# Row turns moved among the first products, and the remainder columns put first in each pair

## The chip, the core and the metric

The kernel runs on one core of one Trainium2 chip. The metric is the device time of one execution in microseconds. "Before" is the median of nine executions. The span of a profile is the time from the first to the last recorded instruction of one profiled execution; about 1.8 us of that execution's own time lie outside it.

## The reference

```
qkv = matmul(x, w_qkv)          # x: (16, 512, 768) f32, w_qkv: (768, 2304) f32
q, k, v = qkv[..., :768], qkv[..., 768:1536], qkv[..., 1536:]
out = stack([q, k, v])          # (3, 16, 512, 768) f32
```

It is one product of 8192 rows by 768 by 2304 columns, with the result split into three equal column groups.

## The kernel before, in words

**Tiling.** The 8192 rows are 32 pairs of two 128-row tiles, pairs numbered from 0. The contraction of 768 is six k-tiles of 128 (KT = 6, KH = 3); k-tile j holds every sixth row of the weights. The 2304 columns are two groups q = 0, 1 of 1024 columns (each two blocks c = 0, 1 of CB = 512) and 256 remainder columns (REM) between them.

**Pairs 0 to 2, direct.** While the weights arrive, these pairs are computed plainly in bf16: `block(q, c, w, groups, cast_next)` runs the products of one column block for all six row tiles, with `groups` as the written-out order of (k-tiles, row tiles). Their rows are loaded as they lie (`load_rows`), cast to bf16 by `cast_rows` (half of each row tile on DVE, half on ACT, or both on DVE with `two=False`), and turned by `turn_rows`: six PE transposes against the identity `eye` into a PSUM bank, then two copies into `xb`. `busy(n)` issues n products of zeros on PE. `cast_k(j)` casts one weight k-tile of the first block. `rem(p)` computes the 256 remainder columns of a pair: twelve 256-column matmuls, one ACT copy to `orem`, one store on SP's queue.

**Pairs 3 to 31, seven products.** For these the two row tiles, the two halves of the contraction and the two blocks of a column group make a two by two by two block product, computed with seven products (Strassen's scheme) for each q. The sums of weights (`sum_w`) and of rows (`sums_x`, on POOL) are fp32r; products 1 and 2 are bf16 and direct. The next pair's rows come in by `load_x` (four quarters, two on SP's queue and two on another), are turned on DVE in 32 by 32 blocks (`transpose`), cast by POOL to `xb` (`round_x`) and summed. `two(a, b, early)` is one pair, with quads a and b for q = 0 and 1. Its order on PE is: product 1 of a and b, `rem`, product 2 of both, product 6 of both, products 5, 7 of a, 5, 7 of b, then 4, 3 of a and 4, 3 of b. `early()` issues the next pair's transposes and sums and the loads of the pair after it. Products 1, 6, 7 and 4 share one PSUM bank per quad (`u.x`), copied out by ACT between them; products 5 and 3 share another (`u.y`), which DVE adds into the output after product 7 and again after product 3. `store_quad` issues two stores per quad on SP's queue. `last(a, b)` is pair 31 with finer stores.

**What sets the order.** The engines' orders are as written; each engine and each issuing queue runs its own list in order and waits on semaphores. Every transfer is given one of eight completion semaphores in turn, and the program makes a transfer's issue wait for the landing of the transfer eight places earlier. PSUM has eight banks, taken in turn (`ps_pool`, bufs=8); row buffers `xin` have three, outputs `o` five, `orem` two.

**Lines of the profile.** L212 products of the seven-product loop; L262 remainder products; L385 direct products; L167 transposes on PE; L365 products of zeros; L145/L149 DVE and L147 ACT halves of casts and turned copies; L413 `cast_k`; L426/L427 casts of the remainder weights; L130 DVE transpose; L175 POOL cast; L226, L233, L239, L243 ACT copies after products 1, 6, 7, 4; L230, L240, L246 DVE adds after products 2, 7, 3; L272/L273 copy and store of `rem`; L89 weight loads; L141 row loads; L126 quarters of `load_x`; L253/L254 and L257/L258 stores of q = 0 and 1.

Of the kernel before, what the change touches and what calls it, by code (L numbers as in the profile page):

```python
# [10 lines left out]
def kernel(  # L11
# [20 lines left out]
    nc = tc.nc  # L32
    P = 128
# [3 lines left out]
    K = H  # L37
    N3 = w_qkv.shape[1]
    KT = K // P
    KH = KT // 2  # L40
    KC = K // 4
    NP = M // (2 * P)
    CB = 512
    REM = N3 - 4 * CB
    Q_OFF = (0, 2 * CB + REM)
    R_OFF = 2 * CB
    fp32 = mybir.dt.float32
    f32r = mybir.dt.float32r
    bf16 = mybir.dt.bfloat16
    ident = mybir.ActivationFunctionType.Identity  # L50
# [9 lines left out]
    tq_pool = ctx.enter_context(tc.tile_pool(name="tq", bufs=2))  # L60
# [6 lines left out]
    xb_pool = ctx.enter_context(tc.tile_pool(name="xb", bufs=4))  # L67
    rem_pool = ctx.enter_context(tc.tile_pool(name="rem", bufs=1))
    s_pool = ctx.enter_context(tc.tile_pool(name="s", bufs=2))
    ps_pool = ctx.enter_context(tc.tile_pool(name="ps", bufs=8, space=bass.MemoryType.PSUM))  # L70
# [4 lines left out]
    eye = w_pool.tile([P, 176], bf16, name="eye")[:, :P]  # L75
    w_rem = [w_pool.tile([P, KH, REM], bf16, name="w_rem0"), None]

    b1 = [w_pool.tile([P, KT, CB], bf16, name=f"b1_{q}") for q in range(2)]
# [8 lines left out]
    def load_w(dst, j0, nj, off, cols):  # L87
        rows = w_qkv.rearrange("(p j) n -> p j n", j=KT)
        nc.sync.dma_start(dst, rows[:, j0:j0 + nj, off:off + cols])  # L89

    stage = {}

    def load_blocks(q, c, nj=KH):
        if q == 0:
            t = tq_pool.tile([P, KT, CB], fp32, name="st0", tag="tq")
            for j in range(0, KT, nj):
                load_w(t[:, j:j + nj], j, nj, Q_OFF[q] + c * CB, CB)
            stage[q, 0, c], stage[q, 1, c] = t[:, :KH, :], t[:, KH:, :]
        else:
            for h in range(2):  # L100
                t = st_pool.tile([P, KH, CB], fp32, name="st1", tag="st")
                load_w(t[:], h * KH, KH, Q_OFF[q] + c * CB, CB)
                stage[q, h, c] = t[:]
# [11 lines left out]
    xin, xf, xb, sr = {}, {}, {}, {}  # L115
# [22 lines left out]
    def load_rows(p):  # L138
        xin[p] = xin_pool.tile([P, 2, K], fp32, name="xin")
        rows = x_flat[p * 2 * P:(p + 1) * 2 * P, :]  # L140
        nc.sync.dma_start(xin[p][:], rows.rearrange("(r m) k -> m r k", m=P))  # L141

    def copy_halves(dst, src, two):

        nc.vector.tensor_copy(out=dst[0], in_=src[0])  # L145
        if two:
            nc.scalar.activation(dst[1], src[1], ident)  # L147
        else:
            nc.vector.tensor_copy(out=dst[1], in_=src[1])  # L149

    xc = {}

    def cast_rows(p, two=True):
        src = xin.pop(p)
        xc[p] = s_pool.tile([P, 2, K], bf16, name="xc", tag="s")
        for r in range(2):
            halves = (slice(0, K // 2), slice(K // 2, K))
            copy_halves([xc[p][:, r, n] for n in halves], [src[:, r, n] for n in halves], two)

    def turn_rows(p, two=True):  # L160
        c = xc.pop(p)
        xb[p] = xb_pool.tile([P, KT, 2 * P], bf16, name="xb", tag="xb")
        for r in range(2):
            cols = c[:, r, :].rearrange("m (p j) -> m j p", j=KT)
            ps = ps_pool.tile([P, KT, P], bf16, name="ps")
            for j in range(KT):
                nc.tensor.transpose(ps[:, j, :], cols[:, j, :], eye)  # L167
            ks = (slice(0, KH), slice(KH, KT))
            copy_halves(
                [xb[p][:, n, r * P:(r + 1) * P] for n in ks], [ps[:, n, :] for n in ks], two  # L170
            )

    def round_x(p):
        xb[p] = xb_pool.tile([P, KT, 2 * P], bf16, name="xb", tag="xb")
# [42 lines left out]
    def bank():  # L217
        return ps_pool.tile([P, CB], fp32, name="ps")

    def do(u, n):  # L220
        c11, c12 = u.o[:, 0, :CB], u.o[:, 0, CB:]
        c21, c22 = u.o[:, 1, :CB], u.o[:, 1, CB:]
        if n == 1:
            u.x = bank()
            product(u, 1, u.x, True)
            nc.scalar.activation(c11, u.x[:], ident)  # L226
        elif n == 2:
            u.z = bank()
            product(u, 2, u.z, True)
            nc.vector.tensor_tensor(c11, c11, u.z[:], op=add)  # L230
        elif n == 6:
            product(u, 6, u.x, False)
            nc.scalar.activation(c12, u.x[:], ident)  # L233
        elif n == 5:
            u.y = bank()
            product(u, 5, u.y, True)
        elif n == 7:
            product(u, 7, u.x, False)
            nc.scalar.activation(c22, u.x[:], ident)  # L239
            nc.vector.tensor_tensor(c22, c22, u.y[:], op=add)  # L240
        elif n == 4:
            product(u, 4, u.x, False)
            nc.scalar.activation(c21, u.x[:], ident)  # L243
        elif n == 3:
            product(u, 3, u.y, False)
            nc.vector.tensor_tensor(c12, c12, u.y[:], op=add)  # L246

    def rows_of(s, p, lo, hi):
        return out_flat[s, p * 2 * P:(p + 1) * 2 * P, lo:hi].rearrange("(r m) n -> m r n", m=P)
# [10 lines left out]
    def rem_row(p, r, ps):  # L260
        for j in range(KT):
            nc.tensor.matmul(  # L262
                ps, xb[p][:, j, r * P:(r + 1) * P], w_rem[j // KH][:, j % KH, :],
                start=(j == 0), stop=(j == KT - 1), skip_group_check=True,
            )

    def rem(p):
        ps = ps_pool.tile([P, 2, REM], fp32, name="ps")
        for r in range(2):
            rem_row(p, r, ps[:, r, :])  # L270
        o = or_pool.tile([P, 2, REM], fp32, name="orem")
        nc.scalar.activation(o[:], ps[:], ident)  # L272
        nc.sync.dma_start(rows_of(1, p, R_OFF - H, R_OFF - H + REM), o[:])  # L273

    def two(a, b, early):

        do(a, 1)
        do(b, 1)
        early()
        rem(a.p)  # L280
        do(a, 2)
        do(b, 2)
        do(a, 6)
        do(b, 6)
        do(a, 5)
        do(a, 7)
        do(b, 5)
        do(b, 7)
        do(a, 4)
        do(a, 3)  # L290
        store_quad(a)
        do(b, 4)
        do(b, 3)
        store_quad(b)
# [52 lines left out]
    load_rows(0)  # L347
    nc.scalar.activation(tiny[:], zero[:, :1], ident)
    make_identity(nc, eye)
    load_rows(1)  # L350
    load_blocks(0, 0, 1)
    st_rem = o_pool.tile([P, KT, REM], fp32, name="str", tag="o")
    load_w(st_rem[:], 0, KT, R_OFF, REM)
    load_rows(2)
    load_blocks(0, 1)
    load_blocks(1, 0)
    load_blocks(1, 1)
    load_x(3, nc.sync)
# [16 lines left out]
    def block(q, c, w, groups, cast_next):  # L375


        ps = {}
        for js, tiles in groups:
            for n in tiles:  # L380
                p, r = divmod(n, 2)
                if n not in ps:
                    ps[n] = bank()
                for j in js:
                    nc.tensor.matmul(  # L385
                        ps[n][:], xb[p][:, j, r * P:(r + 1) * P], w[:, j, :],
                        start=(j == 0), stop=(j == KT - 1), skip_group_check=True,
                    )
                if KT - 1 not in js:
                    continue  # L390
                if r == 0:
                    cast_next(p)
                u = quads[q][p]
                nc.scalar.activation(u.o[:, r, c * CB:(c + 1) * CB], ps[n][:], ident)
                if c == 1 and r == 1:
                    store_quad(u)

    def halves(tiles):
        return [(range(h * KH, (h + 1) * KH), tiles) for h in range(2)]


    singles = [((0, ), (0, 1)), ((1, ), (0, 1)), ((0, 1), (2, 3))]
    singles += [((j, ), range(4)) for j in range(2, KT)]

    act, dve = nc.scalar, nc.vector
    def cast_k(j):
        dve.tensor_copy(out=b1[0][:, j, :], in_=stage[0, j // KH, 0][:, j % KH, :])

    def cast_next(q, c, w):
        return lambda p: p < 2 and cast(q, p, c, w, act)  # L410

# [2 lines left out]

    nothing = lambda p: None
    busy(11)
    cast_rows(0)
    turn_rows(0)
    busy(4)
    cast_rows(1)  # L420
    cast_k(0)
    cast_k(1)
    turn_rows(1)
    for j in range(2, KT):
        cast_k(j)
    act.activation(w_rem[1][:], st_rem[:, KH:], ident)  # L426
    dve.tensor_copy(out=w_rem[0][:], in_=st_rem[:, :KH])  # L427
    bt0 = bt_pool.tile([P, KT, CB], bf16, name="bt")
    bt1 = bt_pool.tile([P, KT, CB], bf16, name="bt")

    block(0, 0, b1[0], singles, nothing)
    rem(0)
    rem(1)
    cast_rows(2, False)
    turn_rows(2, False)
    block(0, 0, b1[0], halves((4, 5)), nothing)
    for h in range(2):
        cast(0, h, 1, bt0, dve)
    for n in range(1, 5):
# [61 lines left out]
```

## Time and profile before

| | us |
|---|---|
| median of 9 executions | 362.58 (362.48 to 363.1) |
| the profiled execution, own time | 362.66 |
| its span | 360.9 |
| PE busy (matmuls) | 354.6 |
| DVE, ACT, POOL busy | 224.7, 182.5, 173.8 |
| bytes moved | 108.08 MB, 299 GB/s over the span |
| granted TensorE clock | 1.0 |

Busy time is the sum of an engine's recorded instructions; PE's matmuls are pipelined and their ends are modelled, so 98% does not say that PE ran at its best. In lines of the timeline the columns are start, length, engine, source line, operation, tile written and tile read, shape, count, and in square brackets the idle time of the engine just before with what ended it. A name ending in q (SPq, ACTq) is the engine's issuing queue. Times of single landings come from the trace's records of semaphore updates by the DMA engines.

### The profile page before, as it was taken

To read this page: it belongs to the slowest core of one execution; us is meant where nothing else is said; L and a number is where in the kernel's file an instruction comes from. 1 tells how busy PE (TensorE), PEld (TensorE's weight loads), DVE (VectorE), ACT (ScalarE), POOL (GpSimd) and SP (SyncE) were. 2 spreads that over 40 slices of the span, in tenths; PEclk is the share of its full clock that TensorE was granted. 3 is DMA by queue.
4 is the path that set the end of the run, shared out by engine and by line. 5 is a ranking of instruction groups with operands and counts; after the bars stand their busy time and mean duration, and the time that the engine had idled before them with its cause. 6 is when DMAs were issued, how large, how long until landed. Compare 5 with 4: busy or idle time off the path is not lost.

```text
span 360.9 us, 5253 instructions
## 1 busy us (share of the span) xinstructions
PE 354.6 (98%) x1797; PEld 250.5 (69%) x1797; DVE 224.7 (62%) x239; ACT 182.5 (51%) x304; POOL 173.8 (48%) x180
## 2 busy tenths in 40 slices
PE   8999999999999999999999999999999999999995
PEld 3644577777777777777777777777777777777763
DVE  3489836765566675566675556676556676556642
ACT  4557554545454545444445444545545454545452
POOL 0000961646664445665445665444666444666410
PEclk9999999999999999999999999999999999999999
DMA  7999869988898999999899999988989899999666
GB/s 296 404 389 370 311 226 359 320 294 293 277 329 302 290 275 296 276 317 317 278 286 284 287 299 314 293 276 291 295 280 324 296 300 271 297 272 337 264 262 232
DMA packets 80617, 108.08 MB, mean 299 GB/s; under 512 B 4816, under 2 KB 60368, under 8 KB 80592
## 3 DMA queue, kind: packets, MB, share of 16 engines
q1 hardware_dynamic: 65184, 96.35, 80.9%
q10 hardware_dynamic: 15408, 11.41, 9.6%
q8 instruction: 14, 0.23, 0.3%
q14 instruction: 11, 0.09, 0.1%
HBM read 32.24 MB, written 75.50 MB: 299 GB/s over the span
## 4 chain that ended last, share of the span: by engine, by line
PE 97%; ACT 1%; ACTq 0%; DVE 0%; issue 0%
PE ps L212 75%; PE ps L262 11%; PE ps L385 9%; PE ps L365 1%; PE ps L167 0%; ACT o L243 0%; ACTq L303 0%; ACT xb L147 0%; ACT orem L317 0%; DVE xb L145 0%; ACT xc L147 0%; ACTq L319 0%; DVE zero L346 0%; ACTq L317 0%
## 5 line engine op out<-in xcount | busy, mean ns | idle before, releaser
L212 PE MATMUL ps<-t,s 128*128 128x512 f32 x696 | 173.8, 398 | 0.0
L212 PEld LDWEIGHTS ps<-t,s 128*128 128x128 f32 x696 | 130.7, 188 | 29.8
L175 POOL CAST xb<-xf 128x1536 bf16<-128x1536 f32 x29 | 43.8, 1510 | 167.8 <-DVE xf L130 133.8
L240 DVE TENSOR_TENSOR o<-o,ps 128x512 f32<-128x512 f32 x58 | 39.9, 688 | 91.1 <-ACT o L239 91.1
L130 DVE STREAM_TRANSPOSE xf<-xin 128x1536 f32<-128x1536 f32 x29 | 85.5, 2949 | 3.2 <-DMA out_dram<-orem 2.0
L212 PE MATMUL ps<-b,xb 128*128 128x512 bf16 x348 | 84.9, 380 | 0.0
L239 ACT ACTIVATE o<-ps 128x512 f32<-128x512 f32 x58 | 34.7, 598 | 44.2 <-PE ps L212 44.2
L212 PEld LDWEIGHTS <-xb 128*128 128x128 bf16 x348 | 31.7, 98 | 35.6 <-issue 7.3
L233 ACT ACTIVATE o<-ps 128x512 f32<-128x512 f32 x58 | 34.8, 600 | 42.1 <-PE ps L212 39.4
L246 DVE TENSOR_TENSOR o<-o,ps 128x512 f32<-128x512 f32 x58 | 39.9, 688 | 21.4 <-PE ps L212 20.2
L212 PE MATMUL ps<-b,s 128*128 128x512 f32 x174 | 48.7, 389 | 0.0
L262 PE MATMUL ps<-w_rem,xb 128*128 128x256 bf16 x384 | 47.2, 273 | 0.0
L243 ACT ACTIVATE o<-ps 128x512 f32<-128x512 f32 x58 | 34.7, 598 | 24.1 <-PE ps L212 21.3
L226 ACT ACTIVATE o<-ps 128x512 f32<-128x512 f32 x58 | 34.6, 597 | 23.8 <-DVE o L246 20.6
L262 PEld LDWEIGHTS <-xb 128*128 128x128 bf16 x384 | 37.4, 98 | 11.2 <-issue 0.5
L230 DVE TENSOR_TENSOR o<-o,ps 128x512 f32<-128x512 f32 x58 | 36.5, 670 | 4.9 <-PE ps L212 3.6
L212 PEld LDWEIGHTS ps<-b,s 128*128 128x128 f32 x174 | 32.7, 188 | 6.8
L184 POOL TENSOR_TENSOR s<-s,xf 128x384 fp32r<-128x384 f32 x29 | 30.0, 1035 | 2.3
L183 POOL TENSOR_TENSOR s<-xf 128x384 fp32r<-128x384 f32 x29 | 30.9, 1065 | 0.0
L185 POOL TENSOR_TENSOR s<-xf 128x384 fp32r<-128x384 f32 x29 | 29.5, 1017 | 0.0
L187 POOL TENSOR_TENSOR s<-xf,s 128x384 fp32r<-128x384 f32 x29 | 29.4, 1014 | 0.0
L272 ACT ACTIVATE orem<-ps 128x512 f32<-128x512 f32 x31 | 18.5, 598 | 20.7 <-PE ps L262 20.7
(36 smaller groups left out, 128.7 us busy)
## 6 DMA issues: line engine op xcount, KB each, us to landing
out_dram<-o SPq DMA_DIRECT2D x62, 768.0 KB, 4.9
out_dram<-o SPq DMA_DIRECT2D x65, 256.0 KB, 4.2
xin<-in_x_dram SPq DMA_DIRECT2D x62, 192.0 KB, 6.9
xin<-in_x_dram ACTq DMA_DIRECT2D x54, 192.0 KB, 4.3
out_dram<-orem SPq DMA_DIRECT2D x31, 256.0 KB, 5.8
st<-in_w_qkv_dram SPq DMA_DIRECT2D x6, 768.0 KB, 13.3
xin<-in_x_dram SPq DMA_DIRECT2D x3, 768.0 KB, 5.6
st<-in_w_qkv_dram SPq DMA_DIRECT2D x6, 256.0 KB, 6.0
```

What stands on the lines that cost most here:

```text
L130: nc.vector.transpose(t[:].rearrange("p j (g b) -> p g j b", b=G), xin.pop(p)[:].rearrange("p g (a j) -> p g j a", a=G),)
L175: nc.gpsimd.tensor_copy(out=xb[p][:], in_=xf[p][:])
L212: nc.tensor.matmul(ps[:], lhs[j], rhs[j], start=(start and j == 0), stop=(j == KH - 1), skip_group_check=True,)
L226: nc.scalar.activation(c11, u.x[:], ident)
L230: nc.vector.tensor_tensor(c11, c11, u.z[:], op=add)
L233: nc.scalar.activation(c12, u.x[:], ident)
L239: nc.scalar.activation(c22, u.x[:], ident)
L240: nc.vector.tensor_tensor(c22, c22, u.y[:], op=add)
L243: nc.scalar.activation(c21, u.x[:], ident)
L246: nc.vector.tensor_tensor(c12, c12, u.y[:], op=add)
L262: nc.tensor.matmul(ps, xb[p][:, j, r * P:(r + 1) * P], w_rem[j // KH][:, j % KH, :], start=(j == 0), stop=(j == KT - 1), skip_group_check= ...
L385: nc.tensor.matmul(ps[n][:], xb[p][:, j, r * P:(r + 1) * P], w[:, j, :], start=(j == 0), stop=(j == KT - 1), skip_group_check=True,)
```

## The change

Five things are different.

1. `cast_rows` and `turn_rows` become `cast_row(p, r)` and `turn_row(p, r)`, for one row tile at a time. The instructions are the same.
2. For pair 1, the casts are interleaved with the casts of k-tiles 0 and 1. The turn of its first tile (`third_row`) comes after the products of k-tile 0 with pair 0, and that of its second tile (`fourth_row`) after those of k-tile 1. The casts of the other k-tiles and of the remainder weights are issued inside these functions, so `block` accepts functions among its groups.
3. For pair 2, the cast and turn of its first tile come after the remainder products of pair 0, and those of its second tile after the remainder products of pair 1. The two tiles' products of the first block then run one tile after the other, six k-tiles each, where they ran in two halves of three.
4. The remainder weights are loaded in two transfers instead of one. The other loads keep their order (`load_blocks(0, 1, KH)` passes the value that was the default).
5. In `two`, `rem(a.p)` moves from behind product 1 and `early()` to the front of the pair. This holds for pairs 3 to 30.

```diff
-    def cast_rows(p, two=True):
-        src = xin.pop(p)
-        xc[p] = s_pool.tile([P, 2, K], bf16, name="xc", tag="s")
-        for r in range(2):
...
-    def turn_rows(p, two=True):
-        c = xc.pop(p)
-        xb[p] = xb_pool.tile([P, KT, 2 * P], bf16, name="xb", tag="xb")
-        for r in range(2):
...
+    def cast_row(p, r, two=True):
+        if r == 0:
+            xc[p] = s_pool.tile([P, 2, K], bf16, name="xc", tag="s")
+        halves = (slice(0, K // 2), slice(K // 2, K))
+        copy_halves([xc[p][:, r, n] for n in halves], [xin[p][:, r, n] for n in halves], two)
+
+    def turn_row(p, r, two=True):
+        if r == 0:
+            xb[p] = xb_pool.tile([P, KT, 2 * P], bf16, name="xb", tag="xb")
+        cols = xc[p][:, r, :].rearrange("m (p j) -> m j p", j=KT)
+        ps = ps_pool.tile([P, KT, P], bf16, name="ps")
+        for j in range(KT):
+            nc.tensor.transpose(ps[:, j, :], cols[:, j, :], eye)
...
     def two(a, b, early):
+        rem(a.p)
         do(a, 1)
         do(b, 1)
         early()
-        rem(a.p)
         do(a, 2)
...
-    load_w(st_rem[:], 0, KT, R_OFF, REM)
+    for h in range(2):
+        load_w(st_rem[:, h * KH:(h + 1) * KH], h * KH, KH, R_OFF, REM)
     load_rows(2)
...
-        for js, tiles in groups:
+        for group in groups:
+            if callable(group):
+                group()
+                continue
+            js, tiles = group
...
     busy(4)
-    cast_rows(1)
+    cast_row(1, 0)
     cast_k(0)
+    cast_row(1, 1)
     cast_k(1)
-    turn_rows(1)
-    for j in range(2, KT):
-        cast_k(j)
-    act.activation(w_rem[1][:], st_rem[:, KH:], ident)
-    dve.tensor_copy(out=w_rem[0][:], in_=st_rem[:, :KH])
+
+    def third_row():
+        turn_row(1, 0)
+        cast_k(2)
+
+    def fourth_row():
+        turn_row(1, 1)
+        for j in range(3, KT):
+            cast_k(j)
+        dve.tensor_copy(out=w_rem[0][:], in_=st_rem[:, :KH])
+        act.activation(w_rem[1][:], st_rem[:, KH:], ident)
...
-    block(0, 0, b1[0], singles, nothing)
-    rem(0)
-    rem(1)
-    cast_rows(2, False)
-    turn_rows(2, False)
-    block(0, 0, b1[0], halves((4, 5)), nothing)
+    block(
+        0, 0, b1[0],
+        [((0, ), (0, 1)), third_row, ((1, ), (0, 1)), fourth_row, ((0, 1), (2, 3))]
+        + [((j, ), range(4)) for j in range(2, KT)],
+        nothing,
+    )
+    for p in range(2):
+        rem(p)
+        cast_row(2, p, False)
+        turn_row(2, p, False)
+    block(0, 0, b1[0], [(range(KT), (4, )), (range(KT), (5, ))], nothing)
```

The removed `singles` held the same order of products as the new list, without the two functions.

More of the change, by code (lines that the diff above doesn't have):

```diff
@@ L151 @@
     xc = {}
-    def cast_rows(p, two=True):
-        src = xin.pop(p)
-        xc[p] = s_pool.tile([P, 2, K], bf16, name="xc", tag="s")
-        for r in range(2):
-            halves = (slice(0, K // 2), slice(K // 2, K))
-            copy_halves([xc[p][:, r, n] for n in halves], [src[:, r, n] for n in halves], two)
-    def turn_rows(p, two=True):
-        c = xc.pop(p)
-        xb[p] = xb_pool.tile([P, KT, 2 * P], bf16, name="xb", tag="xb")
-        for r in range(2):
[L164 to L171, printed above, removed]
+    def cast_row(p, r, two=True):
[10 more added lines that the diff above has]
+            nc.tensor.transpose(ps[:, j, :], cols[:, j, :], eye)
+        ks = (slice(0, KH), slice(KH, KT))
+        copy_halves(
+            [xb[p][:, n, r * P:(r + 1) * P] for n in ks], [ps[:, n, :] for n in ks], two
+        )
     def round_x(p):
@@ L349, with load_k @@
     make_identity(nc, eye)
+    st_0 = tq_pool.tile([P, KT, CB], fp32, name="st0", tag="tq")
+    stage[0, 0, 0], stage[0, 1, 0] = st_0[:, :KH, :], st_0[:, KH:, :]
+    def load_k(j):
+        load_w(st_0[:, j:j + 1], j, 1, Q_OFF[0], CB)
     load_rows(1)
-    load_blocks(0, 0, 1)
+    for j in range(KT):
+        load_k(j)
     st_rem = o_pool.tile([P, KT, REM], fp32, name="str", tag="o")
-    load_w(st_rem[:], 0, KT, R_OFF, REM)
+    for h in range(2):
+        load_w(st_rem[:, h * KH:(h + 1) * KH], h * KH, KH, R_OFF, REM)
     load_rows(2)
-    load_blocks(0, 1)
+    load_blocks(0, 1, KH)
     load_blocks(1, 0)
@@ L399, in halves @@
         return [(range(h * KH, (h + 1) * KH), tiles) for h in range(2)]
-    singles = [((0, ), (0, 1)), ((1, ), (0, 1)), ((0, 1), (2, 3))]
-    singles += [((j, ), range(4)) for j in range(2, KT)]
     act, dve = nc.scalar, nc.vector
-    def cast_k(j):
-        dve.tensor_copy(out=b1[0][:, j, :], in_=stage[0, j // KH, 0][:, j % KH, :])
     def cast_next(q, c, w):
@@ L416 @@
     busy(11)
-    cast_rows(0)
-    turn_rows(0)
+    cast_row(0, 0)
+    cast_row(0, 1)
+    turn_row(0, 0)
+    turn_row(0, 1)
     busy(4)
-    cast_rows(1)
+    cast_row(1, 0)
     cast_k(0)
+    cast_row(1, 1)
     cast_k(1)
-    turn_rows(1)
-    for j in range(2, KT):
-        cast_k(j)
-    act.activation(w_rem[1][:], st_rem[:, KH:], ident)
-    dve.tensor_copy(out=w_rem[0][:], in_=st_rem[:, :KH])
+    def third_row():
[7 more added lines that the diff above has]
+        act.activation(w_rem[1][:], st_rem[:, KH:], ident)
     bt0 = bt_pool.tile([P, KT, CB], bf16, name="bt")
     bt1 = bt_pool.tile([P, KT, CB], bf16, name="bt")
-    block(0, 0, b1[0], singles, nothing)
-    rem(0)
-    rem(1)
-    cast_rows(2, False)
-    turn_rows(2, False)
-    block(0, 0, b1[0], halves((4, 5)), nothing)
+    block(
[3 more added lines that the diff above has]
+        nothing,
+    )
+    for p in range(2):
[3 more added lines that the diff above has]
+    block(0, 0, b1[0], [(range(KT), (4, )), (range(KT), (5, ))], nothing)
     for h in range(2):
```

## The prediction

> **What bounds the kernel now.** I read the busy table first, then the forty slices, the stages (busy time by window), and last the timeline where PE is not full.
>
> ```profile
> PE 354.6 (98%) x1797; PEld 250.5 (69%) x1797; DVE 224.7 (62%) x239; ACT 182.5 (51%) x304; POOL 173.8 (48%) x180
> PEclk9999999999999999999999999999999999999999
> 66.20:345.40 279.20, 279.20 (x1405) 205.49 (x1404) 176.47 (x182) 139.96 (x235) 153.51 (x158) 1.00 0.91 292
> ```
>
> In the last line the columns are window, length, busy time of PE, PEld, DVE, ACT, POOL, then clock, DMA share and GB/s. PE has no hole between 66 and 345 us. Busy time alone would not prove it, so I took the spacing of matmul starts in the trace: from one pair's remainder product to the next is 10.74 us in every steady pair, made of 216 ns for each bf16 matmul of 512 columns, 109 ns for 256 columns and 227 ns for fp32r. So the end is set by when PE starts and by the few places where it waits, and the change can gain only where PE waits now. These are before 20 us:
>
> ```profile
> 8.03 0.95 PE L167 MATMUL ps<-eye,xc 128*128 128x128 bf16 x12 [0.57 <-ACT xc L147]
> 17.56 0.33 PEld L385 LDWEIGHTS <-xb 128*128 128x128 bf16 x3 [0.26 <-DVE xb L145]
> ```
>
> PE waits about 0.7 us for the cast rows of pair 1 (start 8.03, the last zero product issued at 7.08 and lasting 0.22) and 0.28 us for the turned rows of pair 2. More than 1 us is not there to be won. What can be lost lies at the hand-over to the seven-product loop, where the transposing engine is late already:
>
> ```profile
> 46.35 0.89 ACTq L126 DMA_DIRECT2D xin<-in_x_dram  x2
> 49.35 0.37 SPq L258 DMA_DIRECT2D out_dram<-o  x1
> ...
> 52.33 2.38 SPq L126 DMA_DIRECT2D xin<-in_x_dram  x2
> 54.81 0.48 SPq L273 DMA_DIRECT2D out_dram<-orem  x1
> ...
> 58.38 3.02 DVE L130 STREAM_TRANSPOSE xf<-xin 128x1536 f32<-128x1536 f32 x1 [1.97 <-DMA out_dram<-orem]
> 63.01 0.69 DVE L240 TENSOR_TENSOR o<-o,ps 128x512 f32<-128x512 f32 x1 [0.44 <-ACT o L239]
> 64.22 0.84 PE L212 MATMUL ps<-b,s 128*128 128x512 f32 x3
> ```
>
> The built program hands out eight completion semaphores in turn, so a transfer's issue waits for the landing of the one eight before it in the program. SP idles from 42.6 to 49.35 with a store of pair 2 in hand: its eighth predecessor is the first ACT-issued quarter of pair 5, issued at 46.35, landed at 49.29 by the landing records. Behind that store, in SP's order, stand two more stores, the remainder store of pair 2 and the two SP quarters of pair 5, which land at 57.58 and 58.09. The transpose then starts at 58.38, 2.0 us after DVE was free, and PE is spared by little: DVE's add of product 7 (L240) at 63.01 must end before product 3 (64.22) may write the same bank.
>
> **What the Trainium skill says.** "Perfetto Trace Analysis", Identifying the Most-Contended Engine: matmul busy share is a poor measure since matmuls are pipelined. That is why I used start spacing. "TensorE: Matmul & The Clock Gate", Back-to-back issue gap: an isolated gap of N/2.4 + 2.5 ns, 216 ns at 512 columns and 109 at 256; the trace has these two (the page's sustained 131 ns for 512 does not appear here). "DMA: Bandwidth & Descriptors", Issuing engines are not separate DMA queues: transfers from SP and ACT share the same 16 engines. The trace agrees so far as it shows it: the two queues together take 90.5% of the 16 engines' span.
>
> **The change, part by part.**
>
> *Pair 1 turned between products.* No matmul, transpose or copy is added; the order changes. The first product now needs turned pair 0 and k-tile 0. Tile 0 lands at 7.51 and its cast ran 7.54 to 7.97; in the new DVE order it follows only the first row's half cast, so it still ends at 7.97, and PE starts at 8.03, exactly where the turn started before. From there, products 24 x 0.216 = 5.18 plus 12 transposes x 0.056 = 0.67. Tile 1's cast ends at 8.65 before PE wants it (8.80). Row 4 is turned 9.23 to 9.57; its DVE copy starts 0.26 after the last transpose issues, 9.77 to 10.13, and the product that wants it could start at 10.00: about 0.18 of wait. End 8.03 + 5.85 + 0.18 = 14.07 against 13.99 before (8.03 + 0.78 + 5.18).
>
> *Remainder weights in two loads.* One SP issue more (the single one took 0.66 us), and every later SP load waits for one landing later: the third pair's rows are issued at 7.53 instead of 6.87. They landed at 14.65 behind about 2 MB that is already queued, so I take no delay; bound 0 to 0.3 us.
>
> *Pair 2 turned among the remainder products.* Remainder of pair 0: 14.07 + 12 x 0.109 = 15.38. Row 1's two DVE casts start at 14.78 (landing) and end at 15.41: PE waits to 15.46, turns to 15.80, remainder of pair 1 to 17.11. Row 2's casts now stand behind row 1's copies on DVE: copies 16.00 to 16.62, casts 16.54 to 17.16, turn 17.21 to 17.55, then 12 x 0.216 to 20.14, with row 2's copies (17.75 to 18.37) under the first six. Before: 20.16. The head sums to -0.02, bounds -0.5 (the waits above vanish and tile 0 comes sooner) to +0.4 (third rows late).
>
> *Remainder first in the loop.* In 28 pairs, 12 matmuls (1.31 us), an ACT copy and an SP store move ahead of six products. In the steady loop PE's sum is the same, also at the switch from fp32r to bf16: at the tail the trace shows 230 ns then 120 for 256 columns, against 230 then 227 for 512, 11 ns over the pace in both. ACT's two copies of product 1 end 1.31 us later, 3.45 us after the pair's start; products 6 want the banks at 3.7 and 4.6. The ACT loads follow them and took 1.0 us, done before product 6's copy at 4.8. SP's quarters stand behind the remainder store (+1 us); their landing led the transpose by about 1.3 us, and the transpose itself may start some 2.9 us late before PE feels it. Cost 0.
>
> *The same at the hand-over.* ACT issues pair 5's quarters after product 1's copies, now 1.31 us later: 47.66, first landing 50.60, second 51.5. The waiting SP store slips from 49.35 to 50.66, with all behind it. The two remainder stores (pairs 2 and 3) now both stand ahead of pair 5's SP quarters: 256 KB more, 0.69 us (58.09 to 58.78 between these two landings before). Last landing 58.09 + 1.31 + 0.69 = 60.09, transpose at 60.38. From its start, 2.92 to the first add, 0.58 and 0.60 to product 7's add, 0.69 for it and 0.05 to PE: 4.84, so product 3 starts at 65.22 instead of 64.22. **PE stalls 1.0 us, once.** Bounds: 0.3 if the extra store hides (59.69), 1.4 if it costs the 0.97 that pair 2's store took between landings, with the issue times (0.85 to 1.2) on top. Pair 6's quarters then land near 68 against a limit of 71, so it does not repeat.
>
> **Sum.** Own time of the profiled execution 362.66 (span 360.9 and 1.8 around it): 362.66 - 0.02 + 1.0 = 363.64. The median of the nine is 0.08 lower, so 363.56; I say **363.6**. A difference of 0.2% (0.73 us) is about what can be told from none.
>
> **Rivals.**
> 1. *Not slower: the late transpose stays covered.* If SP's queue was held by issue and not by bytes, the extra store fits in a hole and the quarters come within 0.9 us of before. For it: the pipe was empty from 45.9 to 48.4. Against: issues at 51 to 54 took 0.85 to 1.2 us each against 0.37 otherwise, so it was backed up. It decides where the transpose starts before 59.37. Time 362.6. Chance 0.26.
> 2. *Faster: the head pays.* First products at 7.6 if tile 0 is cast at once, and no wait at 17.3: up to -0.5 and -0.28, with the hand-over covered: 361.8. Against: tile 0's landing at 7.51. Chance 0.06.
> 3. *Slower throughout: the steady loop loses.* SP's last quarter now waits for the landing of the first store of the pair just finished (issued 0.4 us before the pair's start, landing 3.4 to 4.4 us later), and ACT's chain has 0.2 to 0.9 us of room. If each of 27 pairs loses 0.1 to 0.3 us, 3 to 8 us: 366 to 371. Against: 2.9 us of room at the transpose. Chance 0.06.
>
> The main case has 0.62, its range 363.2 to 364.2, of which 0.04 lies under the 0.2% mark. Together: faster 0.06, same 0.26 + 0.04 = 0.30, slower 0.58 + 0.06 = 0.64. The range takes in the main case and rival 1: 362.4 to 364.4.
>
> **What would show it.** The second column block (weights bt) starts on PE at 20.1 to 20.2. The SP store after the long SP gap is issued near 50.66, not 49.35. The loop's second transpose (pair 5, called while pair 4 is multiplied) starts near 60.4, and the group of fp32r matmuls has one gap of about 1 us ahead of product 3 of pair 4, with a DVE add (product 7) as its releaser; all other pairs stay at 10.74. If that gap is absent and the time is 362.6, rival 1 holds; if the pairs are longer than 10.74, rival 3; if 20.16 becomes 19.5 or less, rival 2.

## The result and the profile after

| | before | after |
|---|---|---|
| median, us | 362.66 (29 executions) | 364.18 (9 executions) |
| ratio | | 1.0039, 95% interval 1.0031 to 1.0047 |
| profiled execution, own time | 362.66 | 364.32 |
| span | 360.9 | 362.5 |
| PE busy | 354.6 | 355.4 |

The changed kernel is 1.5 us slower, by one stall of PE. Of the executions of the kernel before, most lie near 362.6 us and the others up to 363.35, for a reason that is not known, so its median differs a little from one comparison to the next (362.58 to 362.74); its trace is of the lower group. First the windows of the changed kernel, one for each stage (columns as in the prediction: window, length, busy time of PE, PEld, DVE, ACT, POOL, clock, DMA share, GB/s):

```profile
43.50:55.65 12.15, 12.15 (x68) 9.07 (x65) 5.24 (x6) 6.71 (x12) 6.04 (x7) 1.00 0.62 227
55.65:68.05 12.40, 11.00 (x56) 7.83 (x55) 6.82 (x7) 5.18 (x10) 3.81 (x4) 1.00 1.02 345
68.05:346.90 278.85, 278.85 (x1404) 205.36 (x1404) 177.00 (x182) 139.32 (x235) 154.33 (x159) 1.00 0.90 292
```

PE is full in the first and third line. The second line is pair 4, and there PE is busy for 11.00 of 12.40 us. Busy time again hides a little: by the starts of matmuls, pair 4 takes 12.39 us, every later pair to the last full one 10.74 us. So pair 4 is 1.65 us longer than before. Besides, 0.13 us has been lost in the head (what comes before the loop of pairs) by the time that the second column block starts (20.30 against 20.16), and the tail behind PE's last product is 0.11 us shorter. Together that is the 1.67 us by which the span grew.

The list of waits of the changed kernel (engine and line, releaser, total us, times, longest) names what is new:

```profile
DVE xf L130 <- DMA xin<-in_x_dram: 6.6, 3, 4.4
PE ps L210 <- DVE o L238: 1.4, 1, 1.4
```

PE waits exactly once for DVE's add of product 7 (L238; L240 before), and the DVE transpose has waited 4.4 us in one place. The timeline of the changed kernel shows the two as one chain. These lines answer to those of the kernel before in the prediction:

```profile
47.79 0.89 ACTq L126 DMA_DIRECT2D xin<-in_x_dram  x2
50.79 0.37 SPq L256 DMA_DIRECT2D out_dram<-o  x1
...
52.83 2.15 SPq L271 DMA_DIRECT2D out_dram<-orem  x2
55.07 1.72 SPq L126 DMA_DIRECT2D xin<-in_x_dram  x2
...
60.92 3.08 DVE L130 STREAM_TRANSPOSE xf<-xin 128x1536 f32<-128x1536 f32 x1 [4.38 <-DMA xin<-in_x_dram]
63.89 1.27 DVE L228 TENSOR_TENSOR o<-o,ps 128x512 f32<-128x512 f32 x2
65.06 1.29 DVE L238 TENSOR_TENSOR o<-o,ps 128x512 f32<-128x512 f32 x2
65.91 0.93 PE L210 MATMUL ps<-b,s 128*128 128x512 f32 x3 [1.40 <-DVE o L238]
```

Read from the top. ACT issues pair 5's quarters at 47.79 instead of 46.35. The waiting store leaves SP at 50.79 instead of 49.35. Then come two remainder stores where there was one, and only then SP's quarters, at 55.07 instead of 52.33. The transpose starts at 60.92 instead of 58.38, DVE does the adds of products 2 and 7 behind it without a pause, and PE starts product 3 at 65.91, where 64.35 was due (64.22 before, plus the 0.13 us of the head). In this trace, as in those of the kernel before and of all experiments but `loads_late`, the waiting store leaves 0.06 to 0.07 us after ACT's first quarter has landed (here at 50.72); `loads_late` is explained below.

### The profile page after: what moved, and what is told of

Read it like the earlier page. It is cut to its first block, busy times and chain, and to the rows that moved or that the text cites. A ratio compares the mean times of both kernels' runs of the same rounds, so it can differ in the third digit from the quotient of the medians.

```text
span 362.5 us, 5223 instructions
## 1 busy us (share of the span) xinstructions
PE 355.4 (98%) x1797; PEld 250.5 (69%) x1797; DVE 224.9 (62%) x239; ACT 182.1 (50%) x304; POOL 173.9 (48%) x180
## 4 chain that ended last, share of the span: by engine, by line
PE 93%; DMA 3%; DVE 1%; ACT 1%; ACTq 0%; issue 0%; SPq 0%
PE ps L210 72%; PE ps L260 11%; PE ps L396 9%; DMA xin<-in_x_dram 1%; PE ps L371 1%; DMA out_dram<-orem 1%; PE ps L165 1%; DVE o L228 0%; ACT o L241 0%; ACTq L301 0%; ACT orem L315 0%; DVE xb L145 0%; DVE o L238 0%; ACT o L237 0%; ACT o L224 0%
## 5 line engine op out<-in xcount | busy, mean ns | idle before, releaser
L238 DVE TENSOR_TENSOR o<-o,ps 128x512 f32<-128x512 f32 x58 | 39.8, 689 | 88.8 <-ACT o L237 88.8
L210 PE MATMUL ps<-b,xb 128*128 128x512 bf16 x348 | 80.0, 379 | 0.0
```

The costliest lines, as they stand in the source:

```text
L210: nc.tensor.matmul(ps[:], lhs[j], rhs[j], start=(start and j == 0), stop=(j == KH - 1), skip_group_check=True,)
```

## The experiments

Theory A is the prediction's: the only loss is the late transpose at the hand-over, made late by two things that the moved remainder does in pair 3, namely ACT's later loads and one more store ahead of SP's quarters. The rivals were that the new head costs (B), that the new order costs in every pair (C), and that only one of the two causes counts (D, E).

**head_only** is the changed kernel with the old order in each pair:

```diff
-        rem(a.p)
         do(a, 1)
         do(b, 1)
         early()
+        rem(a.p)
```

> The changed kernel with the old order inside each pair (remainder behind product 1 and the loads). Theory A (all of the loss is the one late transpose at the hand-over, made late by the remainder's move): the gap ahead of product 3 of pair 4 is gone, every pair 10.74 us, time 362.7 (362.4 to 362.9), same as before. Rival B (the new head costs): direct columns end later, time 363.2 or more.

Measured: 362.66 us (13 executions) beside 362.60 of before, ratio 1.0, interval 0.9991 to 1.0008. Pair 4 takes 10.74 us. B falls: the new head costs nothing that can be told.

**rem_first_only** is the kernel before with the opposite edit and nothing else.

> The kernel before with nothing but the remainder put first in pairs 3 to 30. Theory A: one gap of 1.4 to 1.7 us ahead of product 3 of pair 4, time 364.1 (363.8 to 364.4). Rival B (head): 362.7 to 363.0 and no gap.

Measured: 364.13 us (5 executions), ratio 1.0044, interval 1.0031 to 1.0057. Pair 4 takes 12.31 us, 1.57 more than before. Its timeline has the same chain:

```profile
60.53 3.05 DVE L130 STREAM_TRANSPOSE xf<-xin 128x1536 f32<-128x1536 f32 x1 [4.30 <-DMA xin<-in_x_dram]
64.66 1.29 DVE L240 TENSOR_TENSOR o<-o,ps 128x512 f32<-128x512 f32 x2
65.50 0.93 PE L212 MATMUL ps<-b,s 128*128 128x512 f32 x3 [1.28 <-DVE o L240]
```

One moved line of code, `rem(a.p)`, is the whole loss, as far as these times can tell.

**pair3_old** is the changed kernel with the old order in pair 3 alone; pairs 4 to 30 keep the remainder first.

```diff
-        rem(a.p)
+        if a.p != NS:
+            rem(a.p)
         do(a, 1)
         do(b, 1)
         early()
+        if a.p == NS:
+            rem(a.p)
```

> The changed kernel, remainder first in pairs 4 to 30, but pair 3 alone in the old order. Theory A: the hand-over is as before, so no gap, and 27 pairs with the remainder first cost nothing: 362.7 (362.4 to 362.9). Rival C (the new order costs a little in each pair, or the gap only moves to the next pair): 363.5 to 364.2.

Measured: 362.60 us (13 executions), ratio 0.9997, interval 0.9988 to 1.0005. The transpose is back at 58.36, and pairs 4 to 30 take 10.74 us. C falls: twenty-seven pairs with the remainder first cost nothing, and it is the one pair at the hand-over that counts.

**loads_first** keeps the remainder first on PE in every pair, and issues the quarters of pair 5 ahead of pair 3's remainder:

```diff
+        if a.p == NS:
+            load_x(a.p + 2, nc.scalar)
         rem(a.p)
         do(a, 1)
```

(and `early()` leaves these loads out for pair 3).

> The changed kernel with remainder first in all pairs on PE, but the four quarters of pair 5 are issued ahead of pair 3's remainder on ACT and SP. Theory A: it is the late loads, not PE's order, so no gap: last quarter lands at 58 or before, time 362.7 (362.4 to 362.9). Rival C (PE's order itself): 364.1, as the changed kernel.

Measured: 362.61 us (13 executions), ratio 0.9996, interval 0.9988 to 1.0004. ACT now issues at 45.08, the waiting store leaves at 48.17, SP's quarters at 51.15, and the last of them lands at 56.91:

```profile
48.17 0.37 SPq L256 DMA_DIRECT2D out_dram<-o  x1
...
51.15 2.39 SPq L126 DMA_DIRECT2D xin<-in_x_dram  x2
53.63 0.48 SPq L271 DMA_DIRECT2D out_dram<-orem  x1
...
57.13 2.97 DVE L130 STREAM_TRANSPOSE xf<-xin 128x1536 f32<-128x1536 f32 x1 [0.69 <-DMA xin<-in_x_dram]
```

So PE's order is not the cause; where the loads stand is. The loss is gone while the moved products stay moved.

**store_behind** and **store_ahead** take the two causes apart. In the first, pair 3's remainder is still computed first, but its store is issued behind SP's quarters; ACT's quarters stay late.

```diff
...
-        rem(a.p)
+        put = rem(a.p, a.p != NS)     # False: returns the store instead of issuing it
         do(a, 1)
         do(b, 1)
         early()
+        if put:
+            put()
```

> The changed kernel, but in pair 3 the remainder's store is issued behind the SP quarters of pair 5; ACT's quarters stay late. Takes away the second part of the delay alone (0.96 us in the changed kernel's trace). Theory A: gap of product 3 of pair 4 shrinks from 1.56 to about 0.6, time 363.2 (362.9 to 363.5). Rival D (only ACT's later issue matters, stores hide): 364.1.

Measured: 363.20 us (20 executions), ratio 1.0013, interval 1.0006 to 1.002. Pair 4 takes 11.17 us, 0.43 too long, of which 0.33 is the gap ahead of product 3: less than the 0.6 expected, because the store had cost more than its own 0.96 us (worked out below).

In the second, pair 3 has the old order on PE and ACT, so that ACT's quarters are early, but the remainder's store is issued ahead of SP's quarters:

```diff
...
+        if a.p == NS:
+            load_x(a.p + 2, nc.scalar, (1, ))    # ACT's two quarters
+            rem(a.p)
+            load_x(a.p + 2, nc.scalar, (0, ))    # SP's two quarters
```

These lines stand behind `early()`; the first `rem(a.p)` is left out for pair 3, and `early()` leaves out its loads.

> The changed kernel, but in pair 3 the old order on PE and ACT (quarters at their old time), with the remainder's store still ahead of the SP quarters of pair 5. Takes away the first part (1.31 us) alone. Theory A: gap about 0.25, time 362.9 (362.6 to 363.2). Rival D: no gap, 362.6. Rival E (only the extra store matters): gap stays near 1.5, 364.1.

Measured: 362.83 us (12 executions), ratio 1.0005, interval 0.9996 to 1.0013: too small for the times. The trace shows it: pair 4 takes 11.09 us, 0.35 too long (0.25 of it the gap ahead of product 3, as expected). This is one execution, and the slowest of the twelve (363.08). The transposes of the two kernels, one line of each timeline (`store_behind` first):

```profile
59.65 3.09 DVE L130 STREAM_TRANSPOSE xf<-xin 128x1536 f32<-128x1536 f32 x1 [3.14 <-DMA xin<-in_x_dram]
```

```profile
59.64 3.10 DVE L131 STREAM_TRANSPOSE xf<-xin 128x1536 f32<-128x1536 f32 x1 [3.03 <-DMA xin<-in_x_dram]
```

D and E both fall by the times: D wanted 364.1 for `store_behind`, E wanted 364.1 for `store_ahead`. Counted from the start of pair 4, each cause alone puts the transpose 1.1 to 1.2 us later than before. Late loads alone cost PE 0.43 us; that the store alone costs it 0.35 is shown by one trace and not by the times. The two do not add up to 1.65 because the first 0.7 us or so of lateness is free; whichever comes second pays in full.

**loads_late** makes the first cause larger: all quarters of pair 5 behind the copies of product 6 in pair 3.

```diff
         do(b, 6)
+        if a.p == NS:
+            load_x(a.p + 2, nc.scalar)
         do(a, 5)
```

(and `early()` leaves these loads out for pair 3).

> The changed kernel with all quarters of pair 5 issued later still, behind the copies of product 6 of pair 3 (about 2.6 us later on ACT). Theory A: the delay goes through one to one, less what the queue of stores catches up: gap of 3.5 to 4.2 instead of 1.56, time 366.5 (366.0 to 367.0), all of it ahead of product 3 of pair 4. Rival C (the gap is not set by these loads): 364.1.

Measured: 365.04 us (4 executions), ratio 1.0063, interval 1.0046 to 1.008; pair 4 takes 13.19 us, 2.45 too long, all ahead of product 3. The direction and the place were right, the size was not: ACT issued 2.6 us later, the transpose started only 0.83 us later (61.75). SP's timeline of this kernel shows why:

```profile
43.10 0.68 SPq L256 DMA_DIRECT2D out_dram<-o  x1
53.42 0.37 SPq L255 DMA_DIRECT2D out_dram<-o  x1
```

The move shifted the count of eight by one place. The 768 KB store that waited in every other kernel now has an eighth predecessor that has long landed, and leaves at 43.10; the next store waits in its place, to 53.42 (ACT's first quarter landed at 53.40). So less stood in front of SP's quarters.

**One line through all of them.** The start of the transpose, counted from the start of pair 4, against the length of pair 4:

| kernel | transpose after pair 4's start, us | pair 4, us | beyond 10.74 | start less 3.6 |
|---|---|---|---|---|
| loads_first | 1.57 | 10.74 | 0 | none |
| pair3_old | 2.79 | 10.74 | 0 | none |
| before | 2.86 | 10.74 | 0 | none |
| head_only | 2.88 | 10.74 | 0 | none |
| store_ahead | 3.92 | 11.09 | 0.35 | 0.32 |
| store_behind | 4.02 | 11.17 | 0.43 | 0.42 |
| rem_first_only | 5.18 | 12.31 | 1.57 | 1.58 |
| after | 5.26 | 12.39 | 1.65 | 1.66 |
| loads_late | 6.12 | 13.19 | 2.45 | 2.52 |

Pair 4 loses nothing as long as the transpose starts 2.88 us or less after it, and from 3.92 us on it loses about one for one; no kernel lies between, and the line from above meets zero at about 3.6 us. A part of the loss is fixed. In the five kernels that stall, the gap ahead of product 3 is 0.25 to 2.32 us, and pair 4 is 0.09 to 0.13 us longer than by this gap, lost in the next few products. The table shows the last step alone, from the transpose to PE; what makes the transpose late is shown by the experiments above. Not tried was to take the transpose out of the way instead, for example with DVE's adds of pair 4 ahead of it in DVE's order.

**dense_head** asks for a version that beats both. It is `loads_first` with the head's waits taken out:

```diff
-    for p in range(2):
-        rem(p)
-        cast_row(2, p, False)
-        turn_row(2, p, False)
+    rem(0)
+    cast_row(2, 0, False)
+    cast_row(2, 1, False)
+    rem(1, lambda: turn_row(2, 0, False))   # called between its two row tiles
+    turn_row(2, 1, False)
...
-        [((0, ), (0, 1)), third_row, ((1, ), (0, 1)), fourth_row, ((0, 1), (2, 3))]
+        [((0, ), (0, 1)), third_and_fourth, ((1, ), (0, 1)), ((0, 1), (2, 3))]
```

> loads_first with the head's remaining PE waits taken out: both tiles of pair 1 turned before k-tile 1's products, and for pair 2 both casts ahead of the copies on DVE, its first tile turned between the two halves of pair 1's remainder products, its second behind them. If the waits seen in the changed kernel's head (0.18 us ahead of the fourth tile's products, about 0.1 to 0.15 us at each turn of pair 2) are all that is left there, the second column block starts at 19.9 to 20.0 instead of 20.2 to 20.3 and the time is 362.3 (362.1 to 362.5), a little under both kernels and under what a comparison can tell. If new waits take their place (copies late behind the casts): 362.6.

Measured: 362.14 us (18 executions) beside 362.74 of before, ratio 0.9982, interval 0.9975 to 0.9989. It is faster than both kernels, by a little, and more clearly than I had expected: all eighteen executions (362.07 to 362.40) lie below the fastest of the kernel before in any comparison (362.42). PE's lines of its head, with no wait in brackets behind the first product:

```profile
8.00 0.59 PE L400 MATMUL ps<-b,xb 128*128 128x512 bf16 x2 [0.48 <-DVE b L421]
8.43 0.83 PE L165 MATMUL ps<-eye,xc 128*128 128x128 bf16 x12
9.10 4.91 PE L400 MATMUL ps<-b,xb 128*128 128x512 bf16 x22
13.85 2.13 PE L260 MATMUL ps<-w_rem,xb 128*128 128x256 bf16 x18
15.81 0.50 PE L165 MATMUL ps<-eye,xc 128*128 128x128 bf16 x6
16.14 0.82 PE L260 MATMUL ps<-w_rem,xb 128*128 128x256 bf16 x6
16.80 0.50 PE L165 MATMUL ps<-eye,xc 128*128 128x128 bf16 x6
17.14 2.75 PE L400 MATMUL ps<-b,xb 128*128 128x512 bf16 x12
19.73 1.46 PE L400 MATMUL ps<-bt,xb 128*128 128x512 bf16 x6
```

The second column block starts at 19.73, 0.43 us sooner than before and 0.57 sooner than in the changed kernel. Each turn now has other products of PE between it and the casts or copies that it needs or feeds.

## Why the prediction was right, and by how much it was off

- *The head.* Forecast -0.02 us, bounds -0.5 to +0.4. The traces show +0.13 at the second column block, of which 0.10 is there already at the first transpose on PE (5.86 against 5.76), because in this execution the first rows landed 0.11 later; the new order itself is left with about 0.03. The times of `head_only` show no difference. The waits stood where they were put: 0.18 us ahead of the fourth tile's products, and a wait of 0.11 us at each turn of pair 2.
- *The loop.* Forecast at no cost, with the transpose's lateness tolerated. Right: 10.74 us from pair 5 on, and `pair3_old` shows it in the time. In most pairs the last quarter lands closer to the transpose than before (about 0.5 us ahead of it, against 1.3), in the direction worked out; in one pair the transpose waited for it (0.34 us) and PE did not feel it.
- *The hand-over.* Forecast a stall of 1.0 us ahead of product 3 of pair 4, through the store that waits for ACT's quarter, two remainder stores and the DVE chain. Each link is in the trace. The store left at 50.79, forecast 50.66; the difference is the head's 0.13.
- *What was mis-sized: the stall, 1.65 instead of 1.0.* The term that failed is what the second remainder store costs the last of SP's quarters: put at 0.69 us, it was 1.17 here. The last quarter landed 9.91 us after the waiting store was issued, against 8.74 before, so at 60.70 and not at 60.09. Pairs of kernels that differ in this store alone say the same: 1.20 (changed kernel and `store_behind`) and 1.08 (`store_ahead` and `pair3_old`). The store's own interval between landings was 0.96 us; 0.69 came from another place in the queue, behind two loads, and 0.97, the interval of pair 2's store, was named as the upper bound and was the right row. Behind the second store the quarters then took 1.55 and 0.75 us against 1.36 and 0.51, and what stood ahead of it came 0.22 us sooner after the waiting store's issue, which hid a part of the error by luck. The rest is smaller: the chain from the transpose to product 3 took 4.99 us, not 4.84, the products behind the stall lost another 0.09, and the transpose started 0.22 us after the landing, not 0.29. The threshold was put at 3.85 us after pair 4's start. With a chain of 4.99 it is 3.7, since product 3 is due 8.70 us after that start; the fixed loss makes it 3.6 in the table.
- *The numbers.* 364.18 lies in the range of 362.4 to 364.4, 0.6 beyond the forecast of 363.6 and at the very top of the main case's own range (363.2 to 364.2). Slower by over 0.2% had the largest chance. The range also took in the case of no loss at all, so lying in it says little by itself; what bears the forecast out is the chain of events in the traces.
- *The rivals.* The covered transpose (rival 1) would have needed a start before the threshold. The empty stretch named in its favour was shorter than said: packets of ACT's quarters moved from 47.4, not 48.4. The faster head (rival 2) was bounded by the landing of k-tile 0 as argued, but `dense_head` shows that 0.4 us could be had there with another order. The slow steady loop (rival 3) did not occur.

## What to carry to other kernels

Where one engine is full, ask of every moved step what it issues: the products cost nothing in their new place, but they made the copies of product 1 on ACT later, and with them two loads that stand behind these copies, by 1.3 us, and a store on SP got ahead of two other loads. Follow such a delay through the issuing queues to the engine that has least room, here a transpose that was 2 us late already, and look at the transition between two phases, where the slack of the steady loop does not hold. When program-wide completion semaphores are given out in turn, a store can wait for a load on another queue that has nothing to do with it; moving the load earlier removed the loss here (`loads_first`). Moving it by one place in the count freed that store and made the next one wait (`loads_late`), so a shift of the count is to be checked in a trace.

## What the runs showed of the hardware that I had not expected

In a loaded queue, a 256 KB store took 0.96 us between landings (pair 3's remainder in the changed kernel, behind pair 2's) where the same store, behind pair 5's two quarters, took 0.69 us in the kernel before. And a 192 KB quarter took 1.55 us behind that store, but 0.75 us behind another quarter. Bytes alone do not price a transfer there; a transfer of the same kind behind the same kind did better here (0.97 us for pair 2's store, behind another store). What sets these intervals was not tried.

After each of the five stalls of 0.25 to 2.32 us, the second fp32r matmul started 305 to 308 ns after the first, where 227 ns is the pace, and the next ones a few ns over it: 0.09 to 0.13 us in all, about the same for every length of the stall. Why was not tried.
